# The last down round of both FFNs in 1024-column groups with seven products in two K pairs, and x transposed for the mixer in delayed steps

## The chip, the core and the metric

One core of one Trainium2 chip. The metric is the device time of one launch in microseconds (us), as the median of several runs; the profile and the trace come from one further execution, taken by the hardware profiler. TensorE is called PE below, VectorE DVE, ScalarE ACT, GpSimd POOL, and SyncE, whose queue issues the weight loads, SP. PSUM is the accumulator memory that PE writes and ACT and DVE read.

## What is computed

One Macaron layer on 256 tokens, width D = 2048, hidden width 5632, all in float32:

```python
def swiglu(h, w_gate, w_up, w_down):
    return (jax.nn.silu(h @ w_gate) * (h @ w_up)) @ w_down
...
x = x + 0.5 * swiglu(rms_norm(x, ffn1_norm), ffn1_w_gate, ffn1_w_up, ffn1_w_down)
x = x + hybrid_mixer(rms_norm(x, mix_norm), w_in, b_gate, conv_w, w_attn_out, w_conv_out, w_out)
x = x + 0.5 * swiglu(rms_norm(x, ffn2_norm), ffn2_w_gate, ffn2_w_up, ffn2_w_down)
return rms_norm(x, final_norm)
```

The change touches the product with `w_down` in both FFNs, and what stands between the first FFN and the mixer: the squares of x for the norm, and x transposed, scaled by the norm's gain and split, as the mixer's stationary operand `xn`.

## The kernel before

**One product.** A float32 product is made of three matmuls of a reduced type, on the operands split into a high part and a rest: high by high, high by rest, rest by high (lines 230 to 232 in a group, 192 to 194 in a 512-column job). The tokens, in two row halves i = 0 and 1 of 128, are the stationary side; 512 weight columns are the moving side.

**Weights.** They come in chunks of 128 x 1024 (512 KB) through SP's queue. For each chunk ACT casts the high part (`hi`, line 907), then DVE subtracts it from the chunk (`lo`, line 908). There are four pooled pairs of buffers for split chunks: the one that PE is at, and three ahead. PE's program calls `flush` once a chunk; that runs one of the pending steps (small pieces of work left over by the step before) and then lets one pair of transposes for a later operand start, if one is due.

**The down product** takes its 44 K tiles of 128 hidden features in three rounds, `ROUNDS` = 0 to 16, 16 to 32, 32 to 44, as the gate and up products fill a ring of transposed hidden tiles. Rounds 0 and 1 run twice `group`: 1024 output columns as two blocks n = 0, 1 of 512, so four accumulators `C[i, n]` in PSUM. K goes by pairs of tiles (two chunks, eight products). In the pairs that `FAST` names (3 and 5 of eight) seven products stand in for the eight: DVE adds four sums of weight tiles (line 880, into the tile `usum`, printed as sacc; two of them at the chunk called b, two at the one called s1), the sums are split like chunks, and four intermediate products M1, M5, M6, M7 are accumulated besides C. M1 takes the fifth of five banks of the pool `pbig`; M5, M7 and M6 take the three banks psS, psT and psV of the pool `patt`, the ones in which all transposes land. From the chunk before the first fast pair until the last pair the transposes are held back for that (`hold_banks`). Behind the last fast pair four steps are pending, called `early`: a copy and eight DVE adds (lines 608 to 614 and 600) that combine the intermediates and add them to x. In the last pair, behind its first chunk (n = 0) and behind its second (n = 1), `group` runs whatever is still pending and then `drain`, which adds the two accumulators of that block to x.

**The last round** (12 K tiles, six pairs) does not use `group`. `down_last` runs four `wide_job`s of 512 columns, each with two accumulators and 72 matmuls (six chunks); in the second FFN the fourth is `last_job`, which finishes one row half ahead of the other. What `residual` returns runs behind a job: `add` (lines 465, 466: x += 0.5 acc), then `row_square` (line 124), whose ACTIVATE on ACT writes the squares, which nobody reads, over the accumulator just read, and their sum into `ssq`. Behind each job of the first FFN, `turn_one` then runs as four pending steps, one a chunk: two transposes of x into psT or psV, and `split_col` (lines 105, 106). In the second FFN `residual` also multiplies by the final gain (`grow`, line 471), which SP loads into one buffer (line 503) ahead of each job. An ACT table load (line 627) stands behind the first of the four jobs.

**Banks.** `pbig` hands out its five banks in the order in which they come free. ACT, DVE and SP each work in order; a row waits for the one ahead of it.

Of the kernel before, what the change touches and what calls it, by code (L numbers as in the profile page):

```python
# [28 lines left out]
WARM = 11  # L29
FAST = (3, 5)  # L30
RING = 16
LOAD_AHEAD = 6
# [19 lines left out]
def macaron_kernel(ctx: ExitStack, tc: tile.TileContext, xt, gf, cst, wg1, wu1, wd1, win, wv, wao,  # L52
# [159 lines left out]

    def group(wa, wb, k0, pairs, src, fast, xsum, early, drain):

# [21 lines left out]
        def pe(parts):  # L236
            get = iter(parts)
            for p in range(pairs):
# [28 lines left out]
                for n in range(2):  # L267
                    hi, lo, _ = next(get)
                    if first:
                        for i in range(2):  # L270
                            C[i, n] = psum_big("pv")
                    for j, half in enumerate((one, two)):
                        for i in range(2):
                            product(C[i, n], operand(k + j, i), hi, lo, half, first and j == 0, last and j == 1)
                    if fast and p == fast[0] - 1 and n == 0:
                        hold_banks(True)
                    if last:
# [170 lines left out]

    def turn_one(m, gain):

        tag = ("psT", "psV")[m % 2]
        ps = patt.tile([P, 4 * P], F32, name=tag, tag=tag)
        for i in range(2):
            nc.tensor.transpose(ps[:, i * P:(i + 1) * P], x[:, i, m * P:(m + 1) * P], ident)
        split_col(xn[:, m, :], ps[:, 0:T], vec(gain, m))

    def residual(nb, factor, tag, gain):
# [3 lines left out]
        def add(pv):  # L461
            for i, acc in pv.items():
                if factor is None:
                    nc.vector.tensor_add(x[:, i, cols], acc, x[:, i, cols])
                else:
                    nc.vector.scalar_tensor_tensor(x[:, i, cols], acc, factor, x[:, i, cols],
                                                   op0=ALU.mult, op1=ALU.add)
                if tag is not None:
                    row_square(tag, i, nb, acc)
                if tag == "fin":  # L470
# [3 lines left out]
        if tag == "f2":  # L474
# [7 lines left out]
            return [done]  # L482
        if tag is None or tag == "fin":
            return [add]
        return [add, lambda _: None] + [lambda _, m=m: turn_one(m, gain) for m in range(4 * nb, 4 * nb + 4)]

# [50 lines left out]
    def ffn(tag, wg, wu, wd, gain_next, next_tag):  # L537
# [16 lines left out]

        def hidden(q, t):

            k0 = next(a for a, b in ROUNDS if a <= t < b)
            p = (t - k0) // 2
            slot = H_SUMS + 2 * FAST.index(p) if p in FAST and k0 != ROUNDS[-1][0] else None
            r = t % RING  # L560
            turns.append(turn(lambda e, i: gbuf[:, i, (2 * q + e) * P:(2 * q + e + 1) * P],
                              phase["ring"][:, r:r + 2, :], None, slot, delay=2))

# [26 lines left out]
        def gu_last(n_block):  # L590
            def drain(C, n):
                for i in range(2):
                    (gate, up)[n](i, C[i, n], slice(0, NW))
                if n == 1:
                    for q in range(2):
                        hidden(q, 4 * n_block + 2 * q)
            steps.append(group(wg[n_block], wu[n_block], 0, ND // 2, lambda k: xn[:, k, :], (), None, None, drain))
# [3 lines left out]

        def down(r):
            k0, k1 = ROUNDS[r]
            for n1 in (0, 2):
                cols = [slice((n1 + n) * NW, (n1 + n + 1) * NW) for n in range(2)]

                def early(M, cols=cols):
                    return [lambda: (nc.scalar.copy(part[0], M[1]), into(0, cols[0], M[1], 0.5)),
                            lambda: (nc.vector.tensor_add(part[1], M[6], part[0]),
                                     nc.vector.tensor_add(part[2], M[5], part[1]),  # L610
                                     into(0, cols[1], part[2], -0.5)),
                            lambda: (nc.vector.tensor_add(part[3], M[7], part[1]),
                                     into(1, cols[0], part[3], 0.5)),
                            lambda: (nc.vector.tensor_add(part[2], M[5], part[3]),
                                     into(1, cols[1], part[2], -0.5))]

                def drain(C, n, cols=cols):
                    for i in range(2):
                        into(i, cols[n], C[i, n], 0.5)
                steps.append(group(wd[n1], wd[n1 + 1], k0, (k1 - k0) // 2, lambda k, k0=k0: ring((k0 + k) % RING),  # L620
                                   FAST, sums_at(H_SUMS), early, drain))
# [16 lines left out]
        gu("g", 2)  # L638
        down(0)
        gu("u", 2)  # L640
        gu("g", 3)
        gu("u", 3)
        gu("g", 4)
        down(1)
        gu("u", 4)
# [418 lines left out]
```

## Time and profile before

| | |
|---|---|
| time, median of 3 runs | 2457.06 us (2456.94 to 2457.12) |
| the profiled execution: its time, its span | 2457.2 us, 2455.4 us (1.8 us lie around the span) |
| mean granted clock of TensorE | 0.999 |
| PE busy | 2442.7 us, 99%, 12030 matmuls and transposes |
| DVE busy | 1763.6 us, 72% |
| ACT busy | 1221.7 us, 50% |
| DMA | 468.76 MB, mean 191 GB/s, the busiest queue 59.3% of 16 engines' time |
| chain that ended last | PE 99% |
| first FFN, last round: adds of its first 512-column job, in the timeline | 680.95 us; the mixer's products run by 732.24 us |

A page's busy time of PE comes from matmuls that overlap, so the time that one costs is the distance from a start to the next, read from the timeline, and not its printed duration. A row of the timeline that ends in `[1.00 <-ACT hi L907]` says that its engine had been idle for 1.00 us and what ended that. A row with x3 is three instructions of the same kind, one behind the other, printed as one with their time together.

### The profile page before, as it was taken

The page shows a single profiled execution, that of the slowest core. Times are in us where ns is not written, and L with a number is a line of the kernel's source. Part 1 is how long each engine was busy: PE and PEld are TensorE (multiplying, and loading weights), DVE is VectorE, ACT ScalarE, POOL GpSimd, SP SyncE. Part 2 cuts the span into 40 slices and gives each one's busy share as a digit, 9 for nine tenths or more (in the row PEclk, how much of TensorE's full clock was granted, in tenths as well). Part 3 has the DMA queues.
Part 4 walks back from the last instruction along what each step waited for, and adds up shares of the span by engine and source line. Part 5 has one row for each costly group of instructions (what it writes and reads, how often), then busy time and mean ns, then how long its engine had stood idle before and what let it go on. Part 6 is the DMA issues. An engine that isn't in the chain of part 4 may idle for free.

```text
span 2455.4 us, 31711 instructions
## 1 busy us (share of the span) xinstructions
PE 2442.7 (99%) x12030; PEld 2064.3 (84%) x12030; DVE 1763.6 (72%) x2290; ACT 1221.7 (50%) x1573; POOL 1.9 (0%) x10
## 2 busy tenths in 40 slices
PE   9999999999999999999999999999999999999998
PEld 7888888888888888888888888888888888888887
DVE  6888888878557777655556566666578888887855
ACT  5555545554454444444445455445545554555444
POOL 0000000000000000000000000000000000000000
PEclk9999999999999999999999999999999999999999
DMA  7565565656646565556655555566656556565664
GB/s 233 189 203 191 191 208 186 204 189 214 189 142 227 182 195 190 190 188 191 188 178 171 175 170 181 189 193 184 189 189 200 194 190 207 188 205 189 214 189 154
DMA packets 130841, 468.76 MB, mean 191 GB/s; under 512 B 14464, under 2 KB 14720, under 8 KB 130688
## 3 DMA queue, kind: packets, MB, share of 16 engines
q1 hardware_dynamic: 130256, 466.15, 59.3%
q8 instruction: 94, 1.54, 0.3%
q10 hardware_dynamic: 432, 0.59, 0.1%
q14 instruction: 59, 0.48, 0.1%
HBM read 464.58 MB, written 2.10 MB: 190 GB/s over the span
## 4 chain that ended last, share of the span: by engine, by line
PE 99%; DVE 0%; ACT 0%; DMA 0%; issue 0%; DVEq 0%
PE ps L165 21%; PE pv L230 16%; PE pv L232 16%; PE pv L231 16%; PE ps L166 11%; PE pv L194 3%; PE pv L193 3%; PE pv L192 3%; PE pv L744 1%; PE pv L745 1%; PE pv L746 1%; PE psV L231 0%; PE psT L231 0%; PE psS L231 0%; PE psS L232 0%; PE psV L232 0%
## 5 line engine op out<-in xcount | busy, mean ns | idle before, releaser
L908 DVE TENSOR_TENSOR lo<-w,hi 128x1024 fp32r<-128x1024 f32 (+2 forms) x883 | 1028.7, 1183 | 491.1 <-ACT hi L907 481.1
L907 ACT CAST hi<-w 128x1024 fp32r<-128x1024 f32 (+2 forms) x883 | 887.6, 1018 | 677.6 <-PE pv L232 368.1
L165 PE MATMUL ps<-xn,hi 128*128 128x512 f32 x1744 | 611.8, 394 | 0.0
L166 PE MATMUL ps<-xn,lo 128*128 128x256 f32 x1744 | 487.5, 280 | 0.0
L230 PE MATMUL pv<-hi,xn 128*128 128x512 f32 x1228 | 482.9, 393 | 0.5 <-ACT pv L124 0.4
L231 PE MATMUL pv<-lo,xn 128*128 128x512 f32 x1228 | 478.2, 389 | 0.9 <-DVE lo L908 0.9
L232 PE MATMUL pv<-hi,xn 128*128 128x512 f32 x1228 | 478.7, 390 | 0.0
L165 PEld LDWEIGHTS ps<-xn,hi 128*128 128x128 f32 x1744 | 327.5, 188 | 71.5
L166 PEld LDWEIGHTS ps<-xn,lo 128*128 128x128 f32 x1744 | 327.5, 188 | 0.5
L232 PEld LDWEIGHTS pv<-hi,xn 128*128 128x128 f32 x1228 | 230.5, 188 | 48.7 <-DVE xn L106 0.2
L230 PEld LDWEIGHTS pv<-hi,xn 128*128 128x128 f32 x1228 | 230.6, 188 | 48.0 <-ACT pv L124 0.8
L231 PEld LDWEIGHTS pv<-lo,xn 128*128 128x128 f32 x1228 | 230.7, 188 | 47.8 <-DVE lo L908 1.2
L907 ACT CAST hi<-sacc 128x1024 fp32r<-128x1024 f32 x104 | 109.5, 1053 | 190.1 <-PE pv L232 130.8
L908 DVE TENSOR_TENSOR lo<-sacc,hi 128x1024 fp32r<-128x1024 f32 x104 | 127.2, 1223 | 81.7 <-ACT hi L907 81.7
L232 PE MATMUL pv<-hi,ring 128*128 128x512 f32 x432 | 168.1, 389 | 0.0
L231 PE MATMUL pv<-lo,ring 128*128 128x512 f32 x432 | 168.1, 389 | 0.0
L230 PE MATMUL pv<-hi,ring 128*128 128x512 f32 x432 | 168.1, 389 | 0.0
L192 PE MATMUL pv<-hi,ring 128*128 128x512 f32 x304 | 120.3, 396 | 0.0
L194 PE MATMUL pv<-hi,ring 128*128 128x512 f32 x304 | 118.6, 390 | 0.0
L193 PE MATMUL pv<-lo,ring 128*128 128x512 f32 x304 | 118.4, 390 | 0.0
L230 PEld LDWEIGHTS pv<-hi,ring 128*128 128x128 f32 x432 | 81.1, 188 | 16.9
L231 PEld LDWEIGHTS pv<-lo,ring 128*128 128x128 f32 x432 | 81.1, 188 | 16.9
(198 smaller groups left out, 2522.6 us busy)
## 6 DMA issues: line engine op xcount, KB each, us to landing
w<-in_win SPq DMA_DIRECT2D x218, 512.0 KB, 4.2
w<-in_wu SPq DMA_DIRECT2D x176, 512.0 KB, 4.3
w<-in_wd SPq DMA_DIRECT2D x176, 512.0 KB, 4.1
w<-in_wg SPq DMA_DIRECT2D x175, 512.0 KB, 4.1
w<-in_wco SPq DMA_DIRECT2D x32, 512.0 KB, 4.1
w<-in_wv SPq DMA_DIRECT2D x32, 512.0 KB, 4.3
w<-in_wao SPq DMA_DIRECT2D x32, 512.0 KB, 4.4
w<-in_wo SPq DMA_DIRECT2D x32, 512.0 KB, 3.8
```

The costliest lines, as they stand in the source:

```text
L165: nc.tensor.matmul(ps, hi[:, j * P:(j + 1) * P], r, start=(k == 0), stop=False)
L166: nc.tensor.matmul(ps[:, 0:T], lo[:, j * P:(j + 1) * P], r[:, 0:T], start=False, stop=(k == n - 1))
L192: nc.tensor.matmul(pv, xh, hi[:, cols], start=start, stop=False)
L193: nc.tensor.matmul(pv, xh, lo[:, cols], start=False, stop=False)
L194: nc.tensor.matmul(pv, xl, hi[:, cols], start=False, stop=stop)
L230: nc.tensor.matmul(ps, xh, hi[:, sl], start=start, stop=False)
L231: nc.tensor.matmul(ps, xh, lo[:, sl], start=False, stop=False)
L232: nc.tensor.matmul(ps, xl, hi[:, sl], start=False, stop=stop)
L744: nc.tensor.matmul(pv[i], xh, hi[:, cols], start=(k == 0), stop=False)
L745: nc.tensor.matmul(pv[i], xh, lo[:, cols], start=False, stop=False)
L907: nc.scalar.copy(hi[:, cols], w[:, cols])
L908: nc.vector.tensor_sub(lo[:, cols], w[:, cols], f32(hi[:, cols]))
```

## The change

`down(r, n1)` now also builds the last round. The first FFN runs it as two groups, of columns 0 to 1023 and 1024 to 2047; the second as one group for the first half, then the `wide_job` for block 2 and the `last_job` for block 3 as before. In these groups the pairs 2 and 4 of six are the fast ones (`FAST_END`). Where the round is the last, `drain` calls `residual` for each block, so the squares and the transposing follow from there; `load_gain` moves into the pending steps and behind the drain of n = 0. The transposes for the mixer are no longer pending steps of `turn_one` but entries of `turns`: eight of four transposes (two feature tiles each, in turn through psS, psT and psV) with a delay of two chunks. `gu_last` gives its hidden tiles a delay of 1 in place of 2 and, for the fast pairs, also makes the sums of hidden tiles. The table load stands behind the first group.

```diff
+FAST_END = (2, 4)
...
-    def turn_one(m, gain):
-
-        tag = ("psT", "psV")[m % 2]
-        ps = patt.tile([P, 4 * P], F32, name=tag, tag=tag)
-        for i in range(2):
-            nc.tensor.transpose(ps[:, i * P:(i + 1) * P], x[:, i, m * P:(m + 1) * P], ident)
-        split_col(xn[:, m, :], ps[:, 0:T], vec(gain, m))
...
-        if tag is None or tag == "fin":
+        if tag == "fin":
             return [add]
-        return [add, lambda _: None] + [lambda _, m=m: turn_one(m, gain) for m in range(4 * nb, 4 * nb + 4)]
+
+        def done(pv):
+            add(pv)
+            for m in (4 * nb, 4 * nb + 2):
+                turns.append(turn(lambda q, i, m=m: x[:, i, (m + q) * P:(m + q + 1) * P], xn[:, m:m + 2, :],
+                                  lambda q, m=m: vec(gain, m + q), None, delay=2))
+        return [done]
...
-            slot = H_SUMS + 2 * FAST.index(p) if p in FAST and k0 != ROUNDS[-1][0] else None
+            fast = FAST_END if k0 == ROUNDS[-1][0] else FAST
+            slot = H_SUMS + 2 * fast.index(p) if p in fast else None
...
-        def down(r):
+        def down(r, n1):
...
+                return ([lambda: load_gain(n1)] if last and next_tag == "fin" else []) + t
...
+            def drain(C, n):
+                if last:
+                    residual(n1 + n, 0.5, next_tag, gain_next)[0]({i: C[i, n] for i in range(2)})
+                    if next_tag == "fin" and n == 0:
+                        load_gain(n1 + 1)
+                else:
                     for i in range(2):
                         into(i, cols[n], C[i, n], 0.5)
...
+                               FAST_END if last else FAST, sums_at(H_SUMS), early, drain, last and n1 == 0))
...
         def down_last():
+            down(2, 0)
+            table()
+            if next_tag != "fin":
+                down(2, 2)
+                return
             k0, k1 = ROUNDS[-1]
-            for nb in range(NB):
-                if nb == 1:
-                    steps.append(Step([], lambda _: nc.scalar.preload_act_table(AF.Sqrt), hold=False))
-                if next_tag == "fin":
-                    steps.append(Step([], lambda _, nb=nb: load_gain(nb), hold=False))
-                build = last_job if next_tag == "fin" and nb == NB - 1 else wide_job
+            for nb in (2, 3):
+                steps.append(Step([], lambda _, nb=nb: load_gain(nb), hold=False))
+                build = last_job if nb == NB - 1 else wide_job
```

In the rows below x is the layer's x, pv an accumulator, sacc the tile of the parts and weight sums, and w a chunk of weights; the changed kernel's lines 460, 600, 609 to 615, 921, 922, 106, 107, 125 and 631 are 466, 600, 608 to 614, 907, 908, 105, 106, 124 and 627 of the kernel before.

DVE, the first FFN, from the second of the last round's four 512-column jobs on, before:

```order
L466 SCALAR_TENSOR_TENSOR x<-pv,x 128x512 x2
L908 TENSOR_TENSOR lo<-w,hi 128x1024 x2
L106 SCALAR_TENSOR_TENSOR xn<-psT,cs,xn 128x256
L908 TENSOR_TENSOR lo<-w,hi 128x1024
L106 SCALAR_TENSOR_TENSOR xn<-psV,cs,xn 128x256
L908 TENSOR_TENSOR lo<-w,hi 128x1024
```

and in the change, the end of the first group of that round:

```order
L922 TENSOR_TENSOR lo<-w,hi 128x1024 x3
L600 SCALAR_TENSOR_TENSOR x<-pv,x 128x512
L922 TENSOR_TENSOR lo<-w,hi 128x1024
L610 TENSOR_TENSOR sacc<-psV,sacc 128x512
L611 TENSOR_TENSOR sacc<-psS,sacc 128x512
L600 SCALAR_TENSOR_TENSOR x<-sacc,x 128x512
L613 TENSOR_TENSOR sacc<-psT,sacc 128x512
L600 SCALAR_TENSOR_TENSOR x<-sacc,x 128x512
L615 TENSOR_TENSOR sacc<-psS,sacc 128x512
L600 SCALAR_TENSOR_TENSOR x<-sacc,x 128x512
L460 SCALAR_TENSOR_TENSOR x<-pv,x 128x512 x2
L922 TENSOR_TENSOR lo<-w,hi 128x1024
```

Between the first step's add to x (line 600) and the adds of the accumulators (line 460) one lo and seven adds now stand, where before the two adds of a job stood between los.

ACT, the first FFN's end, where the mixer begins, before (512-wide casts are of the mixer's chunks):

```order
L124 ACTIVATE pv,ssq<-x 128x512 x2
L907 CAST hi<-w 128x512 x2
L105 ACTIVATE xn<-psT,cs 128x256
L907 CAST hi<-w 128x512
L105 ACTIVATE xn<-psV,cs 128x256
```

and in the change:

```order
L609 COPY sacc<-pv 128x512
L921 CAST hi<-w 128x512
L125 ACTIVATE pv,ssq<-x 128x512 x2
L921 CAST hi<-w 128x512
L125 ACTIVATE pv,ssq<-x 128x512 x2
L106 ACTIVATE xn<-psV,cs 128x256 x2
L921 CAST hi<-w 128x512
L106 ACTIVATE xn<-psS,cs 128x256 x2
L921 CAST hi<-w 128x512
L106 ACTIVATE xn<-psT,cs 128x256 x2
```

The squares of both blocks now stand one cast apart, and the first transposed pair (psV) behind all four.

ACT, the second FFN, the end of the last round's first half, before:

```order
L907 CAST hi<-w 128x1024 x2
L627 ACT_TABLE_LOAD
L907 CAST hi<-w 128x1024
L124 ACTIVATE pv,ssq<-x 128x512 x2
L907 CAST hi<-w 128x1024 x6
L124 ACTIVATE pv,ssq<-x 128x512 x2
L907 CAST hi<-w 128x1024 x2
```

and in the change:

```order
L921 CAST hi<-w 128x1024 x4
L609 COPY sacc<-pv 128x512
L125 ACTIVATE pv,ssq<-x 128x512 x2
L921 CAST hi<-w 128x1024
L125 ACTIVATE pv,ssq<-x 128x512 x2
L631 ACT_TABLE_LOAD
L921 CAST hi<-w 128x1024 x3
```

The two pairs of squares, six casts apart before, are one cast apart, with the table load behind them.

## Rows read from the trace of the kernel before

**Rows 1.** The page: busy time by engine, and the chain that ended last.
```profile
PE 2442.7 (99%) x12030; PEld 2064.3 (84%) x12030; DVE 1763.6 (72%) x2290; ACT 1221.7 (50%) x1573; POOL 1.9 (0%) x10
...
PE 99%; DVE 0%; ACT 0%; DMA 0%; issue 0%; DVEq 0%
```

**Rows 2.** Timeline of PE (start us, us): a round 1 group, two `turn` steps, the mixer.
```profile
263.76 0.39 PE L230 MATMUL pv<-hi,ring 128*128 128x512 f32 x1
...
274.64 0.39 PE L230 MATMUL pv<-hi,ring 128*128 128x512 f32 x1
...
666.68 0.60 PE L323 MATMUL psT<-ident,gbuf 128*128 128x128 f32 x4
...
669.88 0.60 PE L323 MATMUL psV<-ident,gbuf 128*128 128x128 f32 x4
...
732.24 0.39 PE L525 MATMUL ps<-xn,hi 128*128 128x512 f32 x1
...
733.63 0.39 PE L525 MATMUL ps<-xn,hi 128*128 128x512 f32 x1
```

**Rows 3.** Timeline of DVE: the end of the same round 1 group.
```profile
261.69 3.50 DVE L908 TENSOR_TENSOR lo<-w,hi 128x1024 fp32r<-128x1024 f32 x3
265.10 0.68 DVE L600 SCALAR_TENSOR_TENSOR x<-pv,x 128x512 f32<-128x512 f32 x1
...
268.88 1.22 DVE L908 TENSOR_TENSOR lo<-w,hi 128x1024 fp32r<-128x1024 f32 x1
...
271.35 1.22 DVE L908 TENSOR_TENSOR lo<-w,hi 128x1024 fp32r<-128x1024 f32 x1
...
273.81 1.28 DVE L600 SCALAR_TENSOR_TENSOR x<-pv,x 128x512 f32<-128x512 f32 x2
```

**Rows 4.** Groups by line (| busy us, mean ns | idle before): adds for the weight sums.
```profile
L880 DVE TENSOR_TENSOR sacc<-sacc,w 128x512 f32<-128x512 f32 x104 | 71.5, 687 | 1.8
```

**Rows 5.** Timeline, all engines: after the first 512-column job of the last round, first layer half.
```profile
677.07 1.28 ACT L627 ACT_TABLE_LOAD   x1
...
680.95 1.28 DVE L466 SCALAR_TENSOR_TENSOR x<-pv,x 128x512 f32<-128x512 f32 x2
...
681.67 0.60 ACT L124 ACTIVATE pv<-x 128x512 f32<-128x512 f32 x1 [1.89 <-DVE x L466]
...
682.21 0.19 ACT L124 ACTIVATION_READ_ACCUMULATOR pv<-x 128x1 f32 x1
...
682.91 1.04 ACT L907 CAST hi<-w 128x1024 fp32r<-128x1024 f32 x1
...
683.98 1.23 DVE L908 TENSOR_TENSOR lo<-w,hi 128x1024 fp32r<-128x1024 f32 x1 [1.75 <-ACT hi L907]
```

**Rows 6.** Chain that ended last, in order of time: one step of `split` at the start.
```profile
10.72 0.48 ACT xn L105
...
12.25 0.89 DVE xn L106 x2
```

**Rows 7.** Timeline: after the first 512-column job of the last round, second FFN.
```profile
2400.35 0.68 DVE L466 SCALAR_TENSOR_TENSOR x<-pv,x 128x512 f32<-128x512 f32 x1
...
2403.02 1.98 ACT L907 CAST hi<-w 128x1024 fp32r<-128x1024 f32 x2
...
2404.09 1.23 DVE L908 TENSOR_TENSOR lo<-w,hi 128x1024 fp32r<-128x1024 f32 x1 [1.00 <-ACT hi L907]
```

**Rows 8.** Timeline: the last gain load and who waits for it.
```profile
2437.64 0.33 SPq L503 DMA_DIRECT2D grow<-in_gf  x1
...
2440.50 0.69 DVE L471 TENSOR_TENSOR sacc<-x,grow 128x512 f32<-128x512 f32 x1 [0.89 <-DMA grow<-in_gf]
```

**Rows 9.** Waits of PE (us in all, times, longest us): longest and shortest of four.
```profile
PE psS L323 <- DVE gbuf L398: 1.7, 1, 1.7
...
PE pv L230 <- ACT pv L124: 0.4, 1, 0.4
```

**Rows 10.** Span and mean granted clock of the core.
```profile
core 0: 2455.4 us, clock 0.999
```

More of the change, by code (lines that the diff above doesn't have):

```diff
@@ L211, in wide_job, with group @@
         return Step(chunks, pe, [lambda q=q: q(held[0]) for q in post], shift=0)
-    def group(wa, wb, k0, pairs, src, fast, xsum, early, drain):
+    def group(wa, wb, k0, pairs, src, fast, xsum, early, drain, must_turn=False):
         chunks = []
@@ L276, in pe @@
                         hold_banks(True)
+                        assert not must_turn or not any(t[1][0][0] == "A" for t in turns)
                     if last:
@@ L467, in add @@
                                                    op0=ALU.mult, op1=ALU.add)
-                if tag is not None:
-                    row_square(tag, i, nb, acc)
+                row_square(tag, i, nb, acc)
                 if tag == "fin":
@@ L553, in up, with hidden @@
                                            op0=ALU.mult, op1=ALU.mult)
-        def hidden(q, t):
+        def hidden(q, t, delay=2):
             k0 = next(a for a, b in ROUNDS if a <= t < b)
             p = (t - k0) // 2
-            slot = H_SUMS + 2 * FAST.index(p) if p in FAST and k0 != ROUNDS[-1][0] else None
+            fast = FAST_END if k0 == ROUNDS[-1][0] else FAST
+            slot = H_SUMS + 2 * fast.index(p) if p in fast else None
             r = t % RING
             turns.append(turn(lambda e, i: gbuf[:, i, (2 * q + e) * P:(2 * q + e + 1) * P],
-                              phase["ring"][:, r:r + 2, :], None, slot, delay=2))
+                              phase["ring"][:, r:r + 2, :], None, slot, delay=delay))
         def exact_over_rough_once(tag):
@@ L595, in drain @@
                     for q in range(2):
-                        hidden(q, 4 * n_block + 2 * q)
+                        hidden(q, 4 * n_block + 2 * q, 1)
             steps.append(group(wg[n_block], wu[n_block], 0, ND // 2, lambda k: xn[:, k, :], (), None, None, drain))
@@ L600, in into, with early @@
             nc.vector.scalar_tensor_tensor(x[:, i, cols], src, factor, x[:, i, cols], op0=ALU.mult, op1=ALU.add)
-        def down(r):
+        def down(r, n1):
             k0, k1 = ROUNDS[r]
[L604 to L617, printed above, removed]
+            last = r == len(ROUNDS) - 1
+            cols = [slice((n1 + n) * NW, (n1 + n + 1) * NW) for n in range(2)]
+            def early(M):
+                t = [lambda: (nc.scalar.copy(part[0], M[1]), into(0, cols[0], M[1], 0.5)),
+                     lambda: (nc.vector.tensor_add(part[1], M[6], part[0]),
+                              nc.vector.tensor_add(part[2], M[5], part[1]),
+                              into(0, cols[1], part[2], -0.5)),
+                     lambda: (nc.vector.tensor_add(part[3], M[7], part[1]),
+                              into(1, cols[0], part[3], 0.5)),
+                     lambda: (nc.vector.tensor_add(part[2], M[5], part[3]),
+                              into(1, cols[1], part[2], -0.5))]
+                return ([lambda: load_gain(n1)] if last and next_tag == "fin" else []) + t
[5 more added lines that the diff above has]
+                else:
@@ L618, in drain @@
                     for i in range(2):
                         into(i, cols[n], C[i, n], 0.5)
-                steps.append(group(wd[n1], wd[n1 + 1], k0, (k1 - k0) // 2, lambda k, k0=k0: ring((k0 + k) % RING),
-                                   FAST, sums_at(H_SUMS), early, drain))
+            steps.append(group(wd[n1], wd[n1 + 1], k0, (k1 - k0) // 2, lambda k: ring((k0 + k) % RING),
+                               FAST_END if last else FAST, sums_at(H_SUMS), early, drain, last and n1 == 0))
@@ L623, in down_last, with table @@
+        def table():
+            steps.append(Step([], lambda _: nc.scalar.preload_act_table(AF.Sqrt), hold=False))
         def down_last():
-            k0, k1 = ROUNDS[-1]
-            for nb in range(NB):
-                if nb == 1:
-                    steps.append(Step([], lambda _: nc.scalar.preload_act_table(AF.Sqrt), hold=False))
-                if next_tag == "fin":
-                    steps.append(Step([], lambda _, nb=nb: load_gain(nb), hold=False))
-                build = last_job if next_tag == "fin" and nb == NB - 1 else wide_job
+            down(2, 0)
[3 more added lines that the diff above has]
+                return
+            k0, k1 = ROUNDS[-1]
+            for nb in (2, 3):
+                steps.append(Step([], lambda _, nb=nb: load_gain(nb), hold=False))
+                build = last_job if nb == NB - 1 else wide_job
@@ L638, in ffn @@
         gu("g", 2)
-        down(0)
+        down(0, 0)
+        down(0, 2)
         gu("u", 2)
@@ L643, in ffn @@
         gu("g", 4)
-        down(1)
+        down(1, 0)
+        down(1, 2)
         gu("u", 4)
```

## The prediction, made before the changed kernel had run

> **What bounds the kernel now.** I read the page first [rows 1]: PE is busy for 99% of the span and the chain that ended last lies on PE for 99%, so the time is the sum of what PE executes, and other engines count only where they make PE wait. Every matmul taken away is therefore won, and every wait of PE that appears is lost. The timeline of PE gives the price of a matmul [rows 2]: from 263.76 to 274.64 us there are 48 of 512 columns, back to back, in a group of round 1, so (274.64 - 263.76) / 48 = 0.2267 us each; a chunk of 12 is 2.72, a K pair 5.44. From the first four transposes to the next at 669.88 there are 12 matmuls and four transposes in 3.20 us, so four transposes take 0.48. A chunk of the mixer takes 733.63 - 732.24 = 1.39.
>
> Then I read DVE and ACT at the end of a group [rows 3], since the change puts such ends where 512-column jobs ended. Here the first of the four early steps adds to x at 265.10, the others follow with a lo (the rest of a chunk) between, and the adds of the accumulators start at 273.81. Counted from 263.76, when PE began the pair behind the last fast one, that is 1.34 and 10.05. One lo costs (265.10 - 261.69) / 3 = 1.14. What follows adds that do squares is in [rows 5]: adds at 680.95, the second square's last part at 682.21 + 0.19 = 682.40, so 1.45 later; the next cast 1.96 and the next lo 3.03 after the adds began. Both squares write into the accumulators, so their banks are not free before that.
>
> **The change part by part.**
>
> *Removed.* Seven products for eight: in each fast pair one product of three matmuls less; three groups of two fast pairs, so 18 matmuls: 12 in the first FFN, 6 in the second. 18 x 0.2267 = **-4.1 us**, certain if PE does not wait. Transposes remain 32 of 128 columns for x, in eights of four instead of sixteens of two; I cost that at nothing, with ends 0 and 8 x 0.48 = 3.8 if each regrouping cost a whole set again, which the equal count speaks against. SP's loads are the same; only the four gain loads move (below).
>
> *Added, hidden.* DVE gets 24 weight sums, each 0.687 us [rows 4], the 24 adds of the early steps, four sets of hidden sums and 12 los of sums; ACT 12 casts for these. A set of hidden sums is five operations of at most 0.687, so under 3.5 us; two such sets an FFN, a pair apart, lie beside pairs that ask two los of DVE, 2.3 of 5.4 us. I cost them, and the hidden tiles that `gu_last` transposes a chunk sooner, at nothing; uncovered, a set would cost at most its excess over 3.2, some 0.3. Over a whole group the rest fits too: a fast pair asks of DVE 3 x 1.14 + 0.6 + 4 x 0.69 = 6.8 us, PE takes 21 x 0.2267 = 4.8 for it, so each fast pair uses up 2.0 us of the lead of three chunks (8.2 us) that the buffers hold. Without that lead each of the six fast pairs would cost PE its 2.0. What decides is the ends of the groups, where the lead is spent already. I follow five of them, with t = 0 where PE begins a group's last pair.
>
> *A, first FFN, between its two groups.* The last fast pair is now directly ahead of the last pair, so all four early steps are emptied ahead of the drain of n = 0; against [rows 3] two los fall out: the adds of C start at 10.05 - 2 x 1.14 = 7.77, the squares end at 7.77 + 1.45 = 9.22. PE's last pair ends at 24 x 0.2267 = 5.44. The next group's first accumulator gets M1's bank, long free; its second gets the bank of C[0,0] and is due three matmuls later, at 6.12. PE waits 9.22 - 6.12 = **3.1**. In round 1 no square stood there, and a pair lay between.
>
> *B, the same end, block n = 1.* Cast at 7.77 + 1.96 = 9.73, lo at 10.80, the adds of n = 1 at 11.94, their squares end at 13.39. PE resumes at 9.22 and has the chunk's other nine matmuls (2.04), the first transposes of x (0.48) and three matmuls into C[0,1] (0.68) before C[1,1] wants the bank of the old C[0,1]. It is there at 12.42: **1.0**.
>
> *C, the second group's first fast pair.* ACT does the second square until 14.0, the table load, 1.28 [rows 5], until 15.3; then cast and lo, and what has queued on DVE behind them: two los 2.28, the split of two transposed tiles 1.5, two sums 1.3, a 512-wide lo 0.6, the next split 1.5, two sums 1.4, the lo of the sums 1.2. From 16.4 that makes 26.2. PE wants it at 23.6: 13.39, the rest of the chunk 2.04, transposes 0.48, the second pair 5.44, the fast pair's first two chunks 1.36 and 0.68, and one matmul 0.23. **2.6**. A split hands over from ACT to DVE in 12.25 - 10.72 = 1.53, plus 0.48 [rows 6] is 2.0 alone; interleaved with ready work I count 1.5 on DVE.
>
> *D, first FFN to mixer.* Casts and los are 512 wide at the end here, so the chain of 8.71 (10.05 - 1.34) loses three los and gains one of 0.6: 5.9, from 0.8: drain at 6.7. Short cast and lo end at 9.3, the adds of n = 1 at 9.9, the last square at 11.85. Only then comes, on ACT, the split of the transposes in psV, 2.0, until 13.9. PE has 5.44 + 2 x 0.48 + 1.39 + 0.48 + 1.39 = 9.66 of work, and then the transposes of the fifth pair of tiles want psV: **4.2**. The next five stretches go at 2.2 each (split and one short cast and lo) against 1.87 (1.39 + 0.48) on PE: **1.5**.
>
> *E, second FFN, group to 512-column job.* The same end as A: **3.1**. Behind it, the multiplies by the gain make cast and lo later, 2.67 and 3.74 after the adds [rows 7], so the lo starts at 11.51 and the adds of n = 1 at 12.65. Their gain load can start only when the multiply of n = 0 has freed the one buffer, at 10.5, and took 2.86 in [rows 8] (2437.64 to 2440.50): there at 13.4, in time. The second square ends at 14.7, table load and cast at 16.6 to 17.6, the lo at 18.9. PE, which stalled until 9.22, has nine matmuls, two chunks and one matmul, 9.22 + 2.04 + 5.44 + 0.23 = 16.9: **2.0**.
>
> The sum: -4.1 + (3.1 + 1.0 + 2.6 + 4.2 + 1.5) + (3.1 + 2.0) = -4.1 + 17.5 = **+13.4**. On the profiled execution's 2457.2 that is 2470.6; the median of the runs is 0.14 lower, so **2470.5**. Ends of the uncertain terms: C and the small part of D between 0 and twice (0 to 8.2 for 4.1), B and the end of E between 0 and 3.0 for 3.0 (chains of estimates): about 3 us each way if half goes together, so 2467 to 2474 for this case alone.
>
> The Trainium skill, "Perfetto Trace Analysis", section "Optimizing Tensor Performance", says that independent matmul groups should rotate through different PSUM banks so that evacuating one overlaps the next one's matmuls. That speaks against a group with five banks in use whose successor needs the second bank at once; by it, if the rotation is enough here, the sum would be the first rival's; if it is not, mine.
>
> **The rivals.**
>
> *R1, the other side: the drains stay covered.* In round 1 the same machinery has no wait: adds at 273.81, 0.68 long, so the bank is free at 274.49, against 274.64 + 3 x 0.2267 = 275.32. If the early steps ran early enough, or the squares did not hold the bank, the seams would be free and -4.1 stay: 2453.0. It decides at one point: C[0,0]'s bank free before t = 6.12 rather than at 9.22. Against it: 10.05 - 1.34 - 2.28 = 6.4 us of DVE work stand between the first early step and the drain, which PE's first chunk of 2.7 covers in part only. Chance 0.05.
>
> *R2, only the first wait of each seam is real* (A, D's 4.2, E's 3.1), because the wait itself gives DVE and ACT the time to restore the lead: -4.1 + 10.4 = +6.3: 2463.4. For it: after a wait of 3.1 the lead is a chunk larger. Against: the engines are in debt by their order, not by capacity. Chance 0.08.
>
> *R3, the clock falls.* The granted clock was 0.999 throughout [rows 10], at the upper level of 2.4 GHz, and PE's longest wait, of four, was 1.7 us [rows 9]. Waits of 3 to 4 us do not occur before, so no row excludes that a fall to 1.2 GHz follows one. If PE then ran at half speed for as long as the gap had lasted, it would lose half of that: 2.1 after the longest (2472.7), 5.2 after all three, 2475.8. Chance 0.09.
> The Trainium skill, "TensorE: Matmul & The Clock Gate", section "HAM oscillation", says that idle gaps between bursts of matmuls can put the clock back. By that, the larger figure holds; no run here shows it.
>
> *R4, the weight loads stand behind the gain load in SP's queue.* The gain load of block 1 waits there for a multiply, and weight loads behind it: if the lead in loads is used up, its 2.9 us is lost once: 2473.4. For: SP works in order; against: two chunks are loaded ahead of the four split. Chance 0.06.
>
> That the change doesn't do what it says I exclude: the order has the 18 matmuls fewer.
>
> **How the numbers follow.** A measurement of this kernel can tell about 0.2%, 4.9 us, from no change: 2452.1 to 2462.0 is the same. My forecast has 0.72, R1 0.05, R2 0.08, R3 0.09, R4 0.06. R1's 2453.0 lies within 0.2%, with a little of it (0.01) beyond; R2 and all else lie above 2462. So faster 0.01, same 0.04, slower 0.95. The range: 2465 leaves out R1 and R2 (0.13), and 2476 takes in R3, R4 and the upper end of the forecast.
>
> **What would show it.** In the changed profile, PE should wait for ACT's squares (line 125) about 3.1 us behind the first group of each FFN's last round, and in the mixer's first chunks its transposes should wait some 4 us for psV's split (line 107). PE's four waits before were between 0.4 and 1.7 us [rows 9]; they should come to 17.5 more in all. PE should have 18 matmuls fewer. DVE should be without a gap at the groups' ends, and the adds of line 460 should follow the early steps with no lo between. I am wrong if the waits stay as they were, if the squares end before PE asks, or if the clock row falls below 0.99.

## The result, and the profile after

The changed kernel takes 2471.84 us (median of 4 runs, 2471.65 to 2472.02), the kernel before beside it 2457.03 (4 runs, 2456.94 to 2457.12): 14.8 us slower, a ratio of 1.006 with a 95% interval of 1.0045 to 1.0075. The forecast was 2470.5 in 2465 to 2476, and slower. The span of the profiled execution grew from 2455.4 to 2469.8 us.

The page of the changed kernel, busy time by engine and the chain that ended last; these answer to [rows 1]:

```profile
PE 2447.0 (99%) x12012; PEld 2065.8 (84%) x12012; DVE 1809.1 (73%) x2370; ACT 1236.0 (50%) x1596; POOL 1.9 (0%) x10
...
PE 97%; DVE 1%; ACT 1%; issue 0%; DMA 0%; DVEq 0%; ACTq 0%
```

PE has the 18 matmuls fewer (12030 - 12012), and yet more busy time, which is a first sign that some matmuls became slower. The chain now leaves PE for DVE and ACT for 2% of the span. The waits of PE in the changed kernel (us in all, times, longest), which answer to [rows 9]:

```profile
PE psV L325 <- DVE xn L107: 4.0, 1, 4.0
PE pv L231 <- ACT pv L125: 3.4, 2, 3.0
PE pv L193 <- ACT pv L125: 3.0, 1, 3.0
PE psS L968 <- DVE gbuf L965: 1.2, 1, 1.2
PE psS L325 <- DVE gbuf L400: 1.0, 1, 1.0
PE pv L232 <- DVE lo L922: 0.9, 1, 0.9
PE pv L194 <- DVE lo L922: 0.5, 1, 0.5
PE psS L232 <- DVE lo L922: 0.2, 1, 0.2
```

Four of these stand in the kernel before as well: the lines of 1.2, 1.0 and 0.9, at the kernel's start, and 0.4 of the 3.4. The three long ones are those forecast: the mixer's transposes wanting psV (4.0, forecast 4.2), and PE behind the squares after the first group of either FFN (3.0 and 3.0, forecast 3.1 each). The small ones forecast behind them are nearly missing: B's 1.0 is not in the list, C's 2.6 is 0.2, the rest of D (1.5) is not there, and the rest of E (2.0) is 0.5. What stands there in their place is seen in the next two views. The timeline of PE at the first of the three (start us, us):

```profile
694.03 0.39 PE L233 MATMUL pv<-hi,ring 128*128 128x512 f32 x1
697.42 0.79 PE L231 MATMUL pv<-hi,ring 128*128 128x512 f32 x1 [3.00 <-ACT pv L125]
...
698.43 0.63 PE L233 MATMUL pv<-hi,ring 128*128 128x512 f32 x1
698.86 0.63 PE L231 MATMUL pv<-hi,ring 128*128 128x512 f32 x1
```

Behind the wait a matmul goes from start to start in 0.43 us (698.86 - 698.43) where [rows 2] had 0.2267. The busy time by stretches of the same kernel shows why; behind the five busy times (PE, its weight loads, DVE, ACT, POOL, each with the number of rows) stands the granted clock as a mean of the stretch (1.00 is the upper level throughout, 0.50 the lower), then the DMA share and GB/s:

```profile
690.00:700.00 10.00, 7.00 (x26) 5.43 (x25) 8.12 (x12) 2.27 (x5) 0.00 (x0) 0.83 0.47 167
700.00:710.00 10.00, 10.00 (x42) 8.15 (x42) 6.29 (x10) 6.35 (x11) 0.00 (x0) 0.83 0.37 105
710.00:720.00 10.00, 9.85 (x44) 7.79 (x43) 9.36 (x13) 5.94 (x7) 0.00 (x0) 1.00 0.56 181
733.00:745.00 12.00, 7.99 (x42) 6.95 (x42) 7.81 (x15) 7.17 (x19) 0.00 (x0) 0.86 0.16 50
2420.00:2430.00 10.00, 7.00 (x25) 5.38 (x24) 8.79 (x14) 2.38 (x5) 0.00 (x0) 0.86 0.28 95
```

Behind each of the three waits the clock fell to the lower level, 1.2 GHz, for some us; the mean over the span is 0.996 against [rows 10]. The Trainium skill, "TensorE: Matmul & The Clock Gate", section "HAM oscillation", says that idle gaps between bursts of matmuls can put the clock back; these rows agree. Adding up how far the starts of PE's rows lie apart beyond the pitch, waits left out, gives 3.1 us in 690 to 712, 1.8 in 733 to 750 and 2.2 in 2420 to 2442. So the ledger of the result is: -4.1 for the matmuls; 3.0 + 0.2 + 4.0 + 3.0 + 0.5 = 10.7 of waits; 3.1 + 1.8 + 2.2 = 7.1 of slow matmuls; together +13.7, of the span's +14.4. The remaining 0.7 is about what PE's rows, read in the same way, lie beyond the pitch outside these three stretches: 0.5 in 712 to 733 and 0.3 in 750 to 1018.

How well DVE and ACT kept to the forecast shows in their timelines at the first seam. PE's last pair of the first group began at t = 0 = 688.14 us (the next group's first matmul at 693.58, less 5.44):

```profile
689.48 0.68 DVE L600 SCALAR_TENSOR_TENSOR x<-pv,x 128x512 f32<-128x512 f32 x1
...
695.92 1.28 DVE L460 SCALAR_TENSOR_TENSOR x<-pv,x 128x512 f32<-128x512 f32 x2
...
700.09 1.28 DVE L460 SCALAR_TENSOR_TENSOR x<-pv,x 128x512 f32<-128x512 f32 x2
```

```profile
697.18 0.19 ACT L125 ACTIVATION_READ_ACCUMULATOR pv<-x 128x1 f32 x1
...
701.34 0.19 ACT L125 ACTIVATION_READ_ACCUMULATOR pv<-x 128x1 f32 x1
...
703.45 1.05 ACT L921 CAST hi<-w 128x1024 fp32r<-128x1024 f32 x1
```

The adds of C start at t = 7.78 (forecast 7.77) and at 11.95 (11.94), the squares that hold the banks end at 9.23 (9.22) and 13.39 (13.39), the cast behind the table load starts at 15.31 (15.3). DVE and ACT were as late as forecast at each of these points; PE was not where I had it, because it ran at half speed.

### The profile page after: what moved, and what is told of

Same layout as the page of the kernel before. It is cut to its first block, busy times and chain, and to the rows that moved or that the text cites. A ratio compares the mean times of both kernels' runs of the same rounds, so it can differ in the third digit from the quotient of the medians.

```text
span 2469.8 us, 31791 instructions
## 1 busy us (share of the span) xinstructions
PE 2447.0 (99%) x12012; PEld 2065.8 (84%) x12012; DVE 1809.1 (73%) x2370; ACT 1236.0 (50%) x1596; POOL 1.9 (0%) x10
## 4 chain that ended last, share of the span: by engine, by line
PE 97%; DVE 1%; ACT 1%; issue 0%; DMA 0%; DVEq 0%; ACTq 0%
PE ps L166 21%; PE pv L231 16%; PE pv L233 16%; PE pv L232 16%; PE ps L167 11%; PE pv L194 2%; PE pv L193 2%; PE pv L195 2%; PE pv L758 1%; PE pv L760 1%; PE pv L759 1%; PE psS L232 1%; PE psV L231 1%; PE psS L233 1%; PE psT L231 1%; PE psV L233 1%
## 5 line engine op out<-in xcount | busy, mean ns | idle before, releaser
L921 ACT CAST hi<-sacc 128x1024 fp32r<-128x1024 f32 x116 | 122.2, 1053 | 208.9 <-PE pv L233 151.2
L231 PE MATMUL pv<-hi,ring 128*128 128x512 f32 x546 | 214.3, 392 | 3.0 <-ACT pv L125 3.0
L232 PE MATMUL pv<-lo,ring 128*128 128x512 f32 x546 | 213.4, 391 | 0.0
L233 PE MATMUL pv<-hi,ring 128*128 128x512 f32 x546 | 213.4, 391 | 0.0
L922 DVE TENSOR_TENSOR lo<-sacc,hi 128x1024 fp32r<-128x1024 f32 x116 | 141.9, 1223 | 86.1 <-ACT hi L921 86.0
L231 PEld LDWEIGHTS pv<-hi,ring 128*128 128x128 f32 x546 | 103.2, 189 | 24.6 <-ACT pv L125 3.4
L233 PEld LDWEIGHTS pv<-hi,ring 128*128 128x128 f32 x546 | 103.0, 189 | 21.8
L232 PEld LDWEIGHTS pv<-lo,ring 128*128 128x128 f32 x546 | 103.1, 189 | 21.1
L166 PE MATMUL ps<-at,hi 128*128 128x512 f32 x256 | 89.5, 392 | 0.0
L166 PE MATMUL ps<-ring,hi 128*128 128x512 f32 x256 | 89.4, 392 | 0.0
```

The lines of the kernel that those rows point to most:

```text
L166: nc.tensor.matmul(ps, hi[:, j * P:(j + 1) * P], r, start=(k == 0), stop=False)
L231: nc.tensor.matmul(ps, xh, hi[:, sl], start=start, stop=False)
L232: nc.tensor.matmul(ps, xh, lo[:, sl], start=False, stop=False)
L233: nc.tensor.matmul(ps, xl, hi[:, sl], start=False, stop=stop)
L921: nc.scalar.copy(hi[:, cols], w[:, cols])
L922: nc.vector.tensor_sub(lo[:, cols], w[:, cols], f32(hi[:, cols]))
```

## The experiments

Two theories stood against each other after this. By the first, DVE and ACT are late by what their own queues set, and PE loses that time in one form or the other: a slow matmul only takes the place of a wait. By the second, the fallen clock is a cost of its own. Each run was compared with the kernel before on the same chip.

**PE kept busy in two of the three waits.**

```diff
+    def keep_warm(n, a, b):
+        ps = patt.tile([P, 4 * P], F32, name="psT", tag="psT")
+        for _ in range(n):
+            nc.tensor.matmul(ps, a, b, start=True, stop=True)
...
                         for i in range(2):
+                            if warm and first and (n, j, i) == (0, 0, 1):
+                                keep_warm(warm, operand(k, 0)[0], hi[:, one])
...
```

The same stands in `wide_job`, for the job behind the second FFN's group.

> The changed kernel, with 13 extra matmuls of 512 columns (13 x 0.2267 = 2.95 us) where PE waited 3.0 us behind the first FFN's first group and behind the second FFN's group; they write a bank that nobody reads, so PE is not idle there. The mixer's seam is left alone. Theory 1 (DVE and ACT are late by an amount that their own queues set; PE loses it either as a wait or as slow matmuls): the granted clock stays up in these two stretches, and the waits that the slow matmuls had covered come back: about 1.0 at the second column block and 2 at the first fast pair, about 2 more in the second FFN. The time stays at 2471.8, within 1.0. Theory 2 (the fallen clock is a cost of its own on top of the waits): the 2.9 and 2.2 us that the trace shows above the pitch behind these two waits are saved and nothing takes their place: 2466.7.

Measured 2473.0 us (2472.3 to 2474.7; ratio 1.0066, 1.0054 to 1.0079), 1.2 above the changed kernel. PE's waits there:

```profile
PE psV L334 <- DVE xn L107: 4.0, 1, 4.0
...
PE psS L239 <- DVE lo L932: 1.5, 1, 1.5
PE pv L193 <- ACT hi L931: 1.3, 1, 1.3
...
PE pv L238 <- ACT pv L125: 1.1, 2, 0.7
PE pv L194 <- DVE lo L932: 0.8, 1, 0.8
```

and PE's timeline at the first seam:

```profile
694.08 3.11 PE L200 MATMUL psT<-hi,ring 128*128 128x512 f32 x13
697.24 0.50 PE L238 MATMUL pv<-hi,ring 128*128 128x512 f32 x1
...
701.41 0.50 PE L238 MATMUL pv<-hi,ring 128*128 128x512 f32 x1 [0.69 <-ACT pv L125]
```

With the clock up behind 694, the missing waits came back, each at its place: B 0.7 (forecast 1.0), C 1.5 (2.6), E's rest 1.3 + 0.8 = 2.1 (2.0). Nothing was gained by the faster clock, so the first theory holds for these two seams and the second falls (it gave 2466.7). The mixer's seam was left alone. The 1.2 above, and not the "within 1.0", is a part of the expectation that failed, and so is the clock: in the profiled execution, the longest of the five (2474.7), it fell later after all, behind the 1.5 and behind the 1.3 and 0.8:

```profile
710.00:720.00 10.00, 8.32 (x29) 6.19 (x28) 9.37 (x12) 6.02 (x7) 0.00 (x0) 0.83 0.56 182
2435.00:2445.00 10.00, 7.98 (x28) 5.92 (x27) 6.99 (x6) 8.17 (x8) 0.00 (x0) 0.83 0.89 320
```

Each of these falls makes eight rows 0.2 us longer, 1.6 in all; without the two this execution would be at 2471.5, beside the changed kernel's 2471.8. That the 1.2 of the median is such a fall as well is not shown, since the other four executions have no trace.

**A wait alone.**

```diff
+    def gap(n):
+        ps = patt.tile([P, 4 * P], F32, name="psS", tag="psS")
+        nc.tensor.transpose(ps[:, 0:P], ident, ident)
+        t = tmp("g")
+        nc.scalar.copy(t[:, 0:P], ps[:, 0:P])
...
+        nc.tensor.transpose(ps[:, 0:P], t[:, 0:P], ident)
...
+        steps.append(Step([], lambda _: gap(0 if tag == "f1" else 2)))
         gu("u", 0)
```

> The kernel before with two waits of PE made by hand and nothing else: ahead of the first up group of each FFN, PE transposes a tile, ACT copies it once (first FFN) or three times in a row (second FFN), and PE transposes the copy, so PE stands still for an estimated 3.5 and 2.1 us, with the following chunks ready. Theory 1 (a wait of this length is enough for the granted clock to fall for some us): rows of 0.43 in place of 0.23 us follow at least the longer one, 2 to 3 us above the pitch; 2457.1 + 5.6 + 2 to 6 = 2465 to 2469. Theory 2 (the clock fell at the seams for another reason): no slow matmuls, 2462.7.

Measured 2464.3 us (2464.2 to 2465.7; ratio 1.003, 1.0019 to 1.0041). PE's timeline at the longer gap:

```profile
60.05 0.27 PE L539 MATMUL psS<-ident 128*128 128x128 f32 x1
63.84 0.48 PE L547 MATMUL psT<-ident,g 128*128 128x128 f32 x1 [3.52 <-ACT g L541]
63.97 0.78 PE L230 MATMUL pv<-hi,xn 128*128 128x512 f32 x1
64.54 0.63 PE L231 MATMUL pv<-lo,xn 128*128 128x512 f32 x1
64.97 0.63 PE L232 MATMUL pv<-hi,xn 128*128 128x512 f32 x1
```

and at the shorter one:

```profile
1787.69 0.33 PE L547 MATMUL psT<-ident,g 128*128 128x128 f32 x1 [1.48 <-ACT g L544]
...
1788.09 0.39 PE L231 MATMUL pv<-lo,xn 128*128 128x512 f32 x1
1788.31 0.40 PE L232 MATMUL pv<-hi,xn 128*128 128x512 f32 x1
```

A wait of 3.5 us, with nothing else changed and the next chunks ready, is followed by matmuls of 0.43; the one of 1.5, for which 2.1 was expected, is not. So the time stays 0.7 under the first theory's range, and above the second theory's 2462.7. Here, where DVE and ACT owe nothing, the fall is a real cost: in this trace, of the longest of the seven executions (2465.7), twelve rows behind the longer gap take 0.2 us more than the pitch, 2.4 in all. In the median the two gaps cost 7.2 us against 5.0 of waits, with the four added transposes in the difference too. So the rival on the clock had its mechanism right; in the changed kernel the fall is paid out of time that PE would have waited, as the run that kept PE busy shows for two of the three seams.

**The fast pairs earlier.**

```diff
-FAST_END = (2, 4)
+FAST_END = (2, 3)
```

> The changed kernel with the fast pairs 2 and 3 of six in place of 2 and 4: a pair lies between the last fast one and the drains, as in round 1, and the fast pairs are neighbours. Theory 1 (the four early steps crowd the drain): the three long waits fall from 3.0, 4.0 and 3.0 to about 1, 2 and 1, and the clock stays at the upper level; in their place the second of two neighbouring fast pairs waits about 1.2 in the first groups (two pairs use up 4 us of the lead and more behind the hidden tiles), and the second group of the first FFN, which starts without its lead, 4 to 5 in all. Sum of waits near 15 against the 4.1 saved: 2468. Theory 2 (only the ends of the groups matter): 2457.0 - 4.1 + about 1 = 2454. Theory 3 (the place of the fast pairs does not matter, DVE's load does): 2471 to 2473, with waits of 3 us and the fallen clock as before.

Measured 2468.7 us (2468.5 to 2470.1; ratio 1.0048, 1.0036 to 1.0061), mean granted clock 0.999. PE's waits:

```profile
PE psS L232 <- DVE lo L922: 3.6, 3, 1.5
PE psV L325 <- DVE xn L107: 1.7, 1, 1.7
PE pv L231 <- ACT pv L125: 1.5, 3, 0.7
PE pv L193 <- ACT hi L921: 1.3, 1, 1.3
...
PE pv L193 <- ACT pv L125: 0.8, 1, 0.8
PE pv L194 <- DVE lo L922: 0.8, 1, 0.8
```

The long waits shrank to 0.4, 1.7 and 0.8 (the line of 1.5 is this 0.4, 0.7 for B and the 0.4 of the kernel before), so the crowded early steps made most of them; but the sums of the fast pairs (psS on lo) now wait three times. That the clock stays up was wrong at one place: behind the longest of these three, 1.5 us, it fell, which the mean of 0.999 does not show.

```profile
710.00:720.00 10.00, 8.33 (x28) 5.86 (x27) 9.82 (x13) 5.87 (x7) 0.00 (x0) 0.83 0.48 146
```

The theory that only ends matter (2454) falls, and so does the one by which the place of the fast pairs does not matter (2471 to 2473).

**The squares later, out of the accumulators.**

```diff
-                row_square(tag, i, nb, acc)
+                if tag == "f2":
+                    row_square(tag, i, nb, acc)
+                else:
+                    sq.append([3, lambda i=i: row_square(tag, i, nb, gbuf[:, i, 0:NW])])
...
```

> The changed kernel, where in the last rounds the squares of x run at least three chunks later than the drain and write to SBUF, not into the accumulators. Theory 1 (the squares hold the bank and stand ahead of casts and splits on ACT): the bank of C[0,0] is free behind its add, 0.77 earlier, so the first wait of a group's end is 2.3 to 2.5 in place of 3.0; the mixer's 4.0 becomes 1.5 and then one or two of under 1; the second FFN 2.4 and under 1. Together near 11 us of waits, less the 4.1: 2464 if the clock stays up, 2466 to 2468 if it still falls behind waits of 2.4. Theory 2 (DVE's queue alone sets the ends, ACT has room): no wait changes by more than 0.8, 2470 to 2472.

Measured 2466.8 us (2466.3 to 2467.8; ratio 1.0039, 1.0026 to 1.0053). PE's waits:

```profile
PE pv L231 <- DVE x L466: 2.2, 1, 2.2
PE pv L193 <- DVE x L466: 2.2, 1, 2.2
PE psV L325 <- DVE xn L107: 1.3, 1, 1.3
```

Both group ends now wait for DVE's add, 0.8 less than for the square, and the mixer's 4.0 is 1.3: there the squares had stood ahead of the splits on ACT. DVE's queue alone, the other theory, does not explain that. The clock still fell behind both of the 2.2. Since the squares moved in time and in place at once, the run does not separate the bank that they held from ACT's order; only the rows that the waits name do.

**Both edits.**

> The two edits together: fast pairs 2 and 3, and late squares into SBUF. Theory 1 (two separate causes of the waits at the ends, the crowded early steps and the squares): no wait at an end above 1 us, the clock at the upper level throughout, and what is left is about 1.2 at each pair of neighbouring fast pairs, some 3 in the mixer's first chunks and under 1 in the second FFN, some 8 in all: 2461. Theory 2 (one of the two edits alone does all there is to do): the time is that of the better of the two. Theory 3 (only the ends of groups matter): 2454.

Measured 2462.2 us (2461.9 to 2462.6; ratio 1.0021, 1.0012 to 1.0029), clock 0.999. No wait of more than 0.6 is left at an end; the longest line is

```profile
PE psS L232 <- DVE lo L932: 3.1, 3, 1.1
```

so the two causes are separate: neither edit alone does it. Alone they brought 3.1 and 5.1 us, together 9.7, 1.5 more than the sum; the clock, which fell once and twice in their traces, does not fall in this one. A third cause remains: with two neighbouring fast pairs the sums wait for their lo in each of the three groups.

**Parts of the change alone.** First the transposing of x alone, with no group in the last rounds:

> The changed kernel without any group in the last rounds: both FFNs go back to 512-column jobs, and only the transposing of x for the mixer in eight delayed sets of four stays. Theory 1 (regrouping the transposes costs nothing, as the prediction had it): 2457.1, within 0.5. Theory 2 (the regrouping holds the 0.6 to 0.8 us by which the changed kernel's span exceeds the sum of its waits, slow matmuls and saved matmuls): 2457.7 to 2457.9. Theory 3 (each regrouped set costs a set again, 8 x 0.48): 2460.9.

Measured 2457.06 us against 2457.13 (ratio 1.0, 0.9991 to 1.0009): the regrouped transposes cost nothing, and the 0.7 us are not theirs either. Then the second FFN's group alone beside them, the first FFN back in 512-column jobs:

> The changed kernel with the first FFN's last round back in 512-column jobs (transposing in steps stays); the second FFN keeps its group. Theory 1 (the seams' losses add, each where it is): 6 matmuls less, -1.4, and the second FFN's end as in the changed kernel, 3.0 of wait, 2.2 of slow matmuls, 0.5 of wait: +4.3, so 2461.4, within 0.7. Theory 2 (the second FFN's loss follows from what the first FFN's seams do, in the weight stream or the lead): -1.4 and nothing else, 2455.7.

Measured 2461.5 us (2461.1 to 2461.7; ratio 1.0018, 1.0009 to 1.0026), +4.4 where +4.3 was expected. The seams add, each is where its rows are, and the first FFN's two seams hold the other 10 us.

**Weight sums on GpSimd,** on top of both edits, with the table load and the last squares moved as well:

```diff
-                add(usum[:, NW:2 * NW], b[:, 0:NW], b[:, NW:2 * NW])
+                (nc.gpsimd.tensor_add if kind == "bp" else add)(usum[:, NW:2 * NW], b[:, 0:NW], b[:, NW:2 * NW])
...
```

> Fast pairs 2 and 3 and late squares, and in the last rounds GpSimd makes two of the four weight sums of a fast pair; besides, the table load stands ahead of the first group, and the last squares and the norm's column come three chunks later in the mixer. DVE's demand for a fast pair falls from 6.8 to 5.4 us against PE's 4.8. Theory 1 (DVE's load is what is left between the two fast pairs): the waits of 3.1 there go, the mixer's 1.5 shrink, and the time is 2457.1 - 4.1 + about 2 = 2455, if an add on GpSimd takes less than the chunk of 2.7 us that it has. Theory 2 (GpSimd is slower than that, or slows DVE): the waits move to the sums, one each at four or six places, 1 to 3 us each: 2464 to 2475.

Measured 2464.0 us (2463.3 to 2466.3; ratio 1.003, 1.0019 to 1.0042): slower than both edits without it (2462.2). The groups by line on POOL:

```profile
L919 POOL TENSOR_TENSOR sacc<-sacc,w 128x512 f32<-128x512 f32 x6 | 10.6, 1763 | 39.7 <-issue 18.2 <-ACT hi L932 12.1 <-ACT gbuf L125 9.5
L914 POOL TENSOR_TENSOR sacc<-w 128x512 f32<-128x512 f32 x6 | 8.8, 1472 | 2344.5 <-DMA w<-in_wd 2339.8 <-DVE lo L933 4.7
```

An add that takes DVE 0.687 us took GpSimd 1.5 to 1.8, under the chunk of 2.7 that I had called enough; but the second sum follows from a first and is cast at once, and PE waited for it at three places, 0.8 for the cast and 0.8 for the lo. My expectation was wrong. To be sure that the other moved pieces were not to blame:

> The kernel of the run with two weight sums on GpSimd, with these sums back on DVE; so fast pairs 2 and 3, late squares, the early table load and the later squares in the mixer. Theory 1 (there GpSimd's adds of 1.5 and 1.8 us made the second sums late, at three places 1.6 us each, and the clock fell behind two of them): the waits at the sums return to about 1.1 at three places, the mixer's 1.5 are 1 at most, the clock stays up: 2460.5, between 2459.5 and 2461.5. Theory 2 (the moved table load and the later squares were at fault there): it stays near 2464.

Measured 2460.4 us (2460.2 to 2460.9; ratio 1.0013, 1.0004 to 1.0022). GpSimd's sums were to blame; the other moved pieces had brought 1.7 us over both edits alone.

**One fast pair a group.** First as the only edit of the changed kernel, `FAST_END = (2,)`:

> The changed kernel with one fast pair a group, the third of six (pair 2), in place of two: 9 matmuls less than the kernel before, -2.0. Theory 1 (crowded ends and two fast pairs on one lead make the loss, not the group as such): three pairs lie between the fast one and the drains, so the early steps are done in time, the ends wait under 0.5, the second group's first fast pair about 1 behind the squares and the table load, the mixer about 1; the clock stays up. Waits of 2 to 3: 2457.5, within 1. Theory 2 (the squares in the accumulators and the drains cost a wait at each end whatever lies ahead): three waits of 1 to 3 us, 2460 to 2464.

Measured 2458.6 us (2458.3 to 2459.1; ratio 1.0006, 0.9997 to 1.0015), 0.1 more than the first theory allowed and well below the second: no wait at an end is above 0.2, and the second group's fast pair waits 0.9. Then with the squares, the table load and the norm's column moved:

> One fast pair a group (pair 2), late squares into SBUF, the table load ahead of the first group, the last squares and the norm's column three chunks later in the mixer. Theory 1: all covers hold, waits of under 1 in all, so the 9 matmuls saved show nearly whole: 2455.4, between 2454.9 and 2456.2, below the kernel before. Theory 2 (some cover that is not seen yet costs as much as the matmuls bring): 2457 or more.

Measured 2456.19 us (2455.99 to 2456.35, 11 runs; the kernel before beside it 2457.15, 2456.81 to 2457.68, 27 runs). Of its PE waits, the longest and the one that is new:

```profile
PE psS L978 <- DVE gbuf L975: 1.2, 1, 1.2
...
PE psT L147 <- DVE rc L140: 0.8, 1, 0.8
```

The 0.8 for the norm's column in the mixer (L147) is the only one above 0.4 that the kernel before does not have. The time is at the upper end of what was expected. It is 15.6 us below the changed kernel and 1.0 below the kernel before; none of its 11 runs reaches the lowest of the 27, but the interval of the ratio, 0.9996 (0.9987 to 1.0005), does not exclude no difference, so that it is faster than the kernel before is not shown. Which of the moved pieces brought the 2.4 us over the plain form, no run isolates.

## Why the prediction was right

**The time and the direction.** 2470.5 against 2471.84. By seams, what PE lost in either form against the forecast: first FFN between its groups 3.0 + 0.2 + 3.1 = 6.3 (A + B + C = 6.7); mixer 4.0 + 1.8 = 5.8 (5.7); second FFN 3.0 + 0.5 + 2.2 = 5.7 (5.1). Together 17.8 against 17.5.

**The saved matmuls and the free transposes.** 18 matmuls fewer stand in the page, and the transposing alone moved nothing (2457.06).

**A, D's first wait, E's first wait:** right in place, cause and size (3.0, 4.0, 3.0), and the times of DVE and ACT behind A are right within 0.02 us. The two edits that take away the causes named (crowded early steps, squares in the accumulators and ahead of the splits) took them away together. One wording was off: the row at 682.21 in [rows 5] closes the first square, not the second; the 1.45 were used as the first one's, which is the one that frees C[0,0].

**The step that failed** is the form of what follows, B, C and the rest of D and E: "*B ... 1.0*", "*C ... 2.6*", 1.5 and 2.0 as waits, and the clock as a rival on top. Only 0.7 us was waited there. The clock fell behind each long wait, as the rival said, but was not on top of the sum: behind the two group ends the slow stretch ran while PE would have stood still. For the mixer, where 1.8 of slow matmuls stand in the place of the 1.5 forecast, that is not shown, since no run kept PE busy there. So the rival's 2475.8, and the 0.09 on it, had the right mechanism with a wrong place in the sum; keeping PE busy showed the waits underneath. Had the waits not been owed, as at the longer gap made by hand, the fall would have cost its own time, 2.4 us there. That the total came within 0.3 of the forecast is in part luck: bare, B and C are 1.4 less than forecast, and the slow stretches that came in their place happened to be about as long as the forecast.

**Small misses.** Once visible, B was 0.7 and C 1.5, together 1.4 less than forecast: PE came to C's lo at t = 24.1 in place of 23.6, and the lo was done at 25.9 in place of 26.2. The gain load was not quite in time: DVE waited 0.3 us for it in the second FFN (at 2431.20); what PE lost by that, no run isolates.

**The rivals.** That the drains stay covered (2453.0) failed at the very point named, the bank of C[0,0], free at 9.23 and wanted at 6.12. That only the three long waits are real (2463.4) looks right in the list of waits, and is wrong: the list leaves out what a fallen clock costs. That weight loads come late behind the gain load in SP's queue (2473.4) cost nothing: no wait of PE is for a load. The Trainium skill, "Perfetto Trace Analysis", section "Optimizing Tensor Performance", lets the evacuation of one group overlap the next one's matmuls by rotating banks; with early steps and squares out of the way the ends do so with waits of at most 0.6, with the same five banks. What was missing was not more banks, but a better order on DVE and ACT and banks that the squares do not hold.

## What to carry to other kernels

Fewer matmuls on a saturated engine pay only where the other engines can prepare what they need: compare their demand with its time at the end of a stage, piece by piece and in queue order, not over the whole (DVE is 73% busy and ACT 50%, and their queues made the long waits here). Look at the granted clock by stretches beside the list of waits, since the mean over the span hides a short fall: a stretch at the lower level may be hiding waits, and keeping the engine busy there then gains nothing, while the cure of the first wait cures both. Work that only a later stage needs (here the squares) does not belong between the read of an accumulator and the next cast, nor in the accumulator's bank.

## What the runs showed of the hardware

In the traces, the first 20 us of the kernel left out, the clock fell behind single waits of 3.0, 4.0 and 3.5 us, behind the two of 2.2, and behind a 1.5 at the second group's first fast pair, in the run that kept PE busy and in the one with the fast pairs earlier. It did not fall behind the 1.5 made by hand, nor behind the 1.7 in the mixer with the fast pairs earlier. Behind waits of 1.3 and 0.8 close together it fell in the run that kept PE busy and did not with the fast pairs earlier; behind 0.8 and 0.8 (cast and lo on GpSimd's sums) it fell at two places of three. What decides between these, the runs do not settle. A mean granted clock of 0.999 stands both over a span without a fall (the kernel before) and over one with a fall (the fast pairs earlier). GpSimd's add of 128 x 512 took 1.47 to 1.76 us, as the profile prints it, against DVE's 0.687.
